# Issuing a weight tile earlier, and cutting modulation pieces into halves, in a two-block f32 transformer kernel

## The chip, the cores and the metric

The kernel runs on one core of a Trainium2 chip. The metric is device time in microseconds (us) of one execution. TensorE is PE in all rows, its weight loads are PEld, VectorE is DVE, ScalarE is ACT, GpSimd is POOL and SyncE is SP. TensorE's clock has two levels, 1.2 and 2.4 GHz; a granted clock of 1.00 in a row is the higher, 0.50 the lower.

## The reference, cut

A sequence of 256 tokens with 1024 features goes through two blocks. The first is a normalisation, a gated mixer, a second normalisation and a mixture of 32 experts of which each token takes four. The second block has two layers whose normalisations are shifted, scaled and gated by modulation vectors, computed as `silu(c) @ ada_w` with `ada_w` of 1024 x 6144 for each layer. Layer 0 mixes with a convolution and a recurrence, layer 1 with stick-breaking attention; each layer ends in an MLP.

```python
proj = h @ w_in                       # 1024 -> qa, ka, va, qb, kb, vb, two gates
lam = exp(sum(lam_q1*lam_k1)) - exp(sum(lam_q2*lam_k2)) + lam_init
out_a = diff_attention(qa, ka, va, lam, lam_init, subln_w)
out_b = chunk_band_attention(qb, kb, vb, rel_bias)
merged = gates[:, :, 0]*(out_a @ w_branch_a) + gates[:, :, 1]*(out_b @ w_branch_b)
...
mod = silu(c) @ ada_w[l] + ada_b[l]   # six vectors of 1024 for each of two layers
```

## The kernel before, in words

**Products.** Every large product is made in f32 precision out of three products of rounded halves. A weight tile of 1024 x 512 (2 MB) is taken in four pairs of 128-row slices. For each pair `wsplit` (L227) has ACT cast the pair (`wh`, L198) and DVE subtract the cast from the pair (`wl`, L199); there are two buffers for `wh` and two for `wl`. `gemm_a` (L238) then makes 12 matmuls of 512 columns from a pair (L254 to L256), 48 from a tile. `gemm_b` (L260) makes 24 matmuls of 256 columns from a pair (L269 to L271), with the weights as the stationary operand.

**Weight tiles.** `wload` (L128, its DMA at L135) brings a tile on SP's queue into a ring of three buffers. The tiles of `w_in` come in the order of their columns: the first (`first_w`, in four parts) and the second (`w_ka`) are issued at the start, the third (`w_va`, columns 1024 to 1535) at L687. Between the second and the third stand SP's small loads: rows of parameters into `raw1` and `raw2` (L158 to L162), `rb` (L163), `lamv` (L166) and two broadcast rows `bcs` (L375). A DMA waits for the one issued eight before it on the same kind of queue; in the order below that is `DMAHW` with a number. The kernel's first products follow the tiles: `qk_block(first_w, 0)`, `qk_block(w_ka, 1)` (tile `qkp`), `v_block(w_va, vA)` (tile `vp`), `qk_block(w_qb, 2)`.

**Uses of the small loads.** PE transposes `raw1` and `raw2` into `pv` (L405, L409), and DVE copies them to `vT` and `abT`. DVE reverses `rb` into `rev`, which POOL's queue writes out (`extd`, L417). DVE and ACT make `lam` from `lamv` (L439 to L447). All of these are released by the end of the first projection. Four passes over `x_tm` with `bcs` (`chain_x`, L419) run between the steps of `v_block`.

**Modulation pieces.** `ada` (L615) is a generator. One piece is 512 columns of `ada_w`: the row `silu_c` against tiles `wa`, into a bank `adp` (L646). Its loads go out on POOL's queue (L622). In the attention stage of layer 1 a tile holds 256 rows (512 KB, `kp` is 2), there are two buffers, and a piece takes four tiles; each tile's load is issued when the tile two before it is used up. Pieces 7 to 11 of layer 1 are made there: `ada1` is advanced once after each of four projections, in the code of the last function, and the fifth piece runs in the code that follows (`proj_out`, then `norm_fm` and the first hidden products of the MLP).

**Order.** The instruction stream of each engine is put in order at build by a scheduler; `tc.issue_after(x)` keeps what stands inside it behind `x`. `fill` holds side work (`chain_x`, `chain_s`) which is advanced by `tick` after each pair.

Of the kernel before, what the change touches and what calls it, by code (L numbers as in the profile page):

```python
# [9 lines left out]
F32 = mybir.dt.float32  # L10
# [62 lines left out]
def tile_kernel(  # L73
# [6 lines left out]
    nc = tc.nc  # L80
# [28 lines left out]
    mark = {}  # L109
# [31 lines left out]
    def wcols(w, c0, ncol, k0=0, kc=8, pool=None, parts=1, pin=False):  # L141
        return wload(w[k0 * 128:(k0 + kc) * 128, c0:c0 + ncol].rearrange("(k p) n -> p k n", p=128),
                     "p (k n) -> p k n", k=kc, pool=pool, parts=parts, pin=pin)
# [3 lines left out]
    raw0 = tmp("raw0", 128)  # L147
    nc.scalar.dma_start(raw0[0:8, :], rows_of(ln_in_g, 8))
    nc.scalar.dma_start(raw0[8:16, :], rows_of(ln_in_b, 8))
    w_ka = wcols(w_in[0], 512, 512)  # L150
    raw1, raw2, rb = [accp.tile([128, 512], F32, tag="a", name=n) for n in ("raw1", "raw2", "rb")]
    raw1, raw2, rb = raw1[:, 0:128], raw2[:, 0:128], rb[0:8, 0:257]
    V.memset(raw1, 0.0)
# [69 lines left out]
                return split(two(xh, c), two(xl, c), v)  # L223
        return f

    hold, ready, deferred = [], [], []

    def wsplit(ws, k, n0):
        if ready:
# [9 lines left out]
    def gemm_a(xh, xl, wk, outs, first=True, last=True):  # L239
        n = len(wk)  # L240
        for i in range(0, n, 2):
            ws, k, n0, _ = wk[i]
            wh, wl = wsplit(ws, k, n0)
            if i == 2:
                while deferred:
                    deferred.pop(0)()
            for j in range(2):
                a = first and i + j == 0
                z = last and i + j == n - 1
                c = wk[i + j][3]  # L250
                for t in range(2):
                    hs = xh[:, c, t * 128:(t + 1) * 128]
                    ls = xl[:, c, t * 128:(t + 1) * 128]
                    T.matmul(outs[t], hs, wh[:, j, :], start=a, stop=False)  # L254
                    T.matmul(outs[t], hs, wl[:, j, :], start=False, stop=False)  # L255
                    T.matmul(outs[t], ls, wh[:, j, :], start=False, stop=z)  # L256
            fill.tick()
# [141 lines left out]
        first_end, first_move = qk_block(first_w, 0)  # L399
    after_v, after_s = mark["V"], mark["S"]  # L400

    with tc.issue_after(first_end):
        vT = const.tile([128, 128], F32, name="vT")
        pv = bank("pv")
        T.transpose(pv[:, 0:128], raw1, ident)  # L405
        V.tensor_copy(vT, pv[:, 0:128])
        abT = const.tile([128, 96], F32, name="abT")
        pv2 = bank("pv2")
        T.transpose(pv2[:, 0:128], raw2, ident)  # L409
        V.tensor_copy(abT, pv2[:, 0:96])  # L410
    spread(ln_in_g, ln_in_b)
    with tc.issue_after(after_v):
        rev = tmp("rev", 384)[0:8]
        V.tensor_copy(rev[:, 0:256], rb[:, 255::-1])
        V.tensor_copy(rev[:, 256:384], rb[:, 0:1].to_broadcast([8, 128]))
        extd = dram.tile([8, 384], F32, name="extd")
        nc.gpsimd.dma_start(extd, rev)  # L417

    def chain_x():  # L419
        for t in range(2):  # L420
            for i, op in enumerate((ALU.mult, ALU.add)):
# [11 lines left out]
        S.activation(bias_a, bias_a, AF.Abs)  # L433
        V.memset(bias_a[0:64, 192:256], -NEG)

    qk_block(w_ka, 1)

    with tc.issue_after(after_v), tc.issue_after(first_move):
        lam = const.tile([128, 1], F32, name="lam")  # L439
        lp = tmp("lp", 128).rearrange("p (a d) -> p a d", a=2)  # L440
        V.tensor_tensor(lp, lamv[:, :, 0, :], lamv[:, :, 1, :], op=ALU.mult)
        le = small("le", 2)
        V.tensor_reduce(le, lp, axis=AX.X, op=ALU.add)
        S.activation(le, le, AF.Exp)
        V.scalar_tensor_tensor(lam, le[:, 0:1], LAM_INIT, le[:, 1:2], op0=ALU.add, op1=ALU.subtract)
        sub8 = const.tile([128, 1], F32, name="sub8")
        V.tensor_scalar(sub8, vT[:, 100:101], 1.0 - LAM_INIT, None, op0=ALU.mult)  # L447
# [151 lines left out]
    def ada(items, late=True):  # L599
        def finish(l, j, acc, tag):  # L600
            v, hf = divmod(j, 2)
            p = bank("ada", tag)
            c = 8 * v + 4 * hf
            for q in range(4):
                T.matmul(p[:, q:q + 1], acc[:, q * 128:(q + 1) * 128], qsel, start=q == 0, stop=q == 3,
                         skip_group_check=True)
            V.tensor_tensor(modT[l][:, c:c + 4], p[:, 0:4], abT[:, 48 * l + c:48 * l + c + 4], op=ALU.add)
            if v in (1, 4) and hf:
                i = v // 3
                V.scalar_tensor_tensor(scl[l][:, i, :], modT[l][:, 8 * v:8 * v + 8], 1.0,  # L610
                                       vT[:, 32 + 16 * i + 8 * l:40 + 16 * i + 8 * l], op0=ALU.add, op1=ALU.mult)

        def flush(h):
            if h[1] // 2 in (2, 5):
                pending.append(h)  # L615
            else:
                finish(*h)

        def load(l, j, i, pin=False):
            w = ada_ring[0](i)  # L620
            r = 128 * ada_ring[2]
            ins = nc.gpsimd.dma_start(w, ada_w_2[l, r * i:r * (i + 1), 512 * j:512 * (j + 1)]  # L622
                                      .rearrange("(k p) n -> p k n", p=128))
            if pin:
                keep(ins)
            return w

        held, got = [], None
        for n, (l, j, tag) in enumerate(items):
            if len(held) > 2:  # L630
                flush(held.pop(0))
            if late and n == len(items) - 1:
                while held:
                    flush(held.pop(0))
                yield
            if got is None:
                got = [load(l, j, i, True) for i in range(2)]
                yield
            kp = ada_ring[2]
            nxt = []  # L640
            pa = bank("adp", tag)
            for i in range(8 // kp):
                for r in range(kp):
                    k = kp * i + r
                    q = 32 * (k % 4)
                    T.matmul(pa[q:q + 32, :], silu_c[:, k:k + 1].to_broadcast([128, 32]), got[i][:, r, :],  # L646
                             start=k < 4, stop=k >= 4, skip_group_check=True)
                if i + 2 < 8 // kp:
                    got.append(load(l, j, i + 2))
                elif ada_ring[1] and n + 1 < len(items):  # L650
                    nxt.append(load(*items[n + 1][0:2], i + 2 - 8 // kp))
            acc = accp.tile([128, 512], F32, tag="a", name="adacc")
            S.copy(acc, pa)
            got = nxt or None
            held.append((l, j, acc, tag))
            yield
        for h in held:
            flush(h)
# [25 lines left out]
        pending.clear()  # L684
        return taken

    w_va = wcols(w_in[0], 1024, 512)  # L687
    fill.add(chain_x())
    v_block(w_va, vA)
    fill.drain()  # L690
# [999 lines left out]
    fill.rate = 1.42  # L1690
    qk_half(0, 0)
    next(ada1, None)
    qk_half(1, 0)
    next(ada1, None)
    keep(S.preload_act_table_set("natural_log_exp_and_others"))
# [3 lines left out]
    qk_half(0, 1)  # L1699
    next(ada1, None)  # L1700
    qk_half(1, 1)
    fill.add(chain_s(1))
    v_half(1)
    fill.drain()
    w_first = proj_out(1, ohl5[:, 0], ohl5[:, 1], w_out_c_2[0], (0, 1), ada1)
    st.close()
# [33 lines left out]
```

## Time and profile before

| | us |
|---|---|
| three runs | 1883.79, 1882.14, 1879.09 |
| median | 1882.14 |
| the profiled execution | 1886.43 |
| its span in the trace | 1884.6 |
| granted TensorE clock over the span | 0.985 |
| busy PE | 1832.9 (97%) |
| busy DVE, ACT, POOL | 842.0, 571.5, 73.9 |

The rows below are from the profiled execution. In a timeline a row has the start, the duration, the engine, the line, the operation and tile, a count of instructions taken together, and in brackets how long the engine stood idle before it and what ended that. PE rows overlap: the time that a matmul takes of PE is the distance from its start to the next one's. In a table by stretch a row has the stretch, its length, the busy time and number of instructions of PE, PEld, DVE, ACT and POOL, the granted clock, the busy share of the 16 DMA engines and what they moved in GB/s.

### The profile page before, as it was taken

How to read it: one execution, taken by the hardware profiler on the slowest of the kernel's cores; microseconds unless marked ns; L12 is line 12 of the kernel's file. 1: busy time of each engine (PE TensorE's matmuls, PEld its weight loads, DVE VectorE, ACT ScalarE, POOL GpSimd, SP SyncE). 2: the span in 40 equal slices, each digit the busy share in tenths (PEclk: the TensorE clock that was granted, in tenths of full speed). 3: DMA queues.
4: the chain of work that ended last, by engine and by line, in shares of the span. 5: the costliest groups of instructions: out<-in, count | busy, mean ns of one | idle time of the engine just before them, and what ended most of it. 6: DMA issues, size and time to landing. Idle time of an engine off the chain costs nothing.

```text
span 1884.6 us, 22815 instructions
## 1 busy us (share of the span) xinstructions
PE 1832.9 (97%) x9419; PEld 1070.7 (57%) x9419; DVE 842.0 (45%) x1521; ACT 571.5 (30%) x934; POOL 73.9 (4%) x101
## 2 busy tenths in 40 slices
PE   6999999999999999999999998999999998999998
PEld 6867743333333333333333333788778865668887
DVE  5775652212131222221222212767755565676666
ACT  3555321011101111101111101554544454564443
POOL 1000000000000000000000000200100011000000
PEclk9999999999999999999999999899999998999999
DMA  8658869999999999999999999774676565434552
GB/s 293 251 192 302 350 250 428 428 427 427 427 428 382 428 427 428 427 428 428 427 428 428 427 428 406 270 256 147 233 263 243 210 232 181 157 134 157 183 202 84
DMA packets 100364, 595.81 MB, mean 316 GB/s; under 512 B 7597, under 2 KB 8066, under 8 KB 75426
## 3 DMA queue, kind: packets, MB, share of 16 engines
q1 hardware_dynamic: 85874, 540.68, 71.2%
q0 software_dynamic: 14352, 53.64, 8.2%
q8 instruction: 75, 1.23, 0.3%
q14 instruction: 31, 0.25, 0.0%
q10 hardware_dynamic: 32, 0.01, 0.0%
HBM read 593.24 MB, written 1.06 MB: 315 GB/s over the span
## 4 chain that ended last, share of the span: by engine, by line
PE 71%; DMA 8%; DVE 3%; issue 3%; ACT 1%; POOL 1%; DVEq 0%; POOLq 0%; ACTq 0%
PE py L980 11%; PE pg L949 10%; PE pu L949 10%; PE hid L285 6%; DMA w<-in_w_exp_in_dram 5%; PE pc L993 4%; PE xg L916 3%; PE acc L254 3%; PE acc L256 3%; PE acc L255 3%; PE hid L287 3%; DMA wa<-in_ada_w_dram 2%; PE adp L646 2%; PE pg L794 1%; PE pu L794 1%
## 5 line engine op out<-in xcount | busy, mean ns | idle before, releaser
L199 DVE TENSOR_TENSOR wl<-w,wh 128x1024 fp32r<-128x1024 f32 x244 | 298.5, 1224 | 217.4 <-ACT wh L198 215.6
L198 ACT CAST wh<-w 128x1024 fp32r<-128x1024 f32 x244 | 256.2, 1050 | 299.7 <-PE acc L256 92.2
L949 PE MATMUL pg<-w,xg 128*64 128x512 f32 x1016 | 260.4, 601 | 1.9 <-DMA w<-in_w_exp_in_dram 1.7
L949 PE MATMUL pu<-w,xg 128*64 128x512 f32 x1016 | 255.6, 592 | 0.0
L980 PE MATMUL py<-w,aTs 128*64 128x512 f32 x1024 | 227.1, 595 | 1.9 <-DMA w<-in_w_exp_out_dram 1.9
L998 DVE TENSOR_TENSOR bcs<-bcs,pc 128x512 f32<-128x512 f32 x124 | 78.1, 683 | 319.5 <-PE pc L993 319.5
L924 DVE TENSOR_SCALAR xg<-xg,gbP 128x128 f32<-128x128 f32 (+1 forms) x68 | 27.3, 401 | 323.9 <-PE xg L916 307.6
L285 PE MATMUL hid<-xhl,wh 128*128 128x512 f32 x448 | 158.7, 398 | 0.0
L949 PEld LDWEIGHTS pu<-w,xg 128*64 128x64 f32 x1016 | 73.0, 137 | 145.8 <-issue 145.8
L980 PEld LDWEIGHTS py<-w,aTs 128*64 128x64 f32 x1024 | 70.7, 137 | 135.6 <-issue 131.8
L949 PEld LDWEIGHTS pg<-w,xg 128*64 128x64 f32 x1016 | 67.0, 137 | 139.3 <-issue 127.8
L287 PE MATMUL hid<-xhl,wl 128*128 128x256 f32 x448 | 125.8, 281 | 0.0
L285 PEld LDWEIGHTS hid<-xhl,wh 128*128 128x128 f32 x448 | 84.2, 188 | 20.7
L254 PE MATMUL acc<-wh,hh 128*128 128x512 f32 x240 | 94.7, 395 | 0.0
L256 PE MATMUL acc<-wh,hh 128*128 128x512 f32 x240 | 93.6, 390 | 0.0
L255 PE MATMUL acc<-wl,hh 128*128 128x512 f32 x240 | 93.6, 390 | 0.0
L974 ACT COPY aTs<-aT 128x512 f32<-128x512 f32 x32 | 18.8, 586 | 231.3 <-PE aT L971 231.3
L287 PEld LDWEIGHTS hid<-xhl,wl 128*128 128x128 f32 x448 | 84.6, 189 | 0.5
L985 ACT COPY ys<-py 128x512 f32<-128x512 f32 x32 | 18.8, 586 | 216.3 <-PE py L980 216.3
L916 PEld LDWEIGHTS xg<-sel,h 128*128 128x128 f32 x544 | 66.7, 196 | 29.6 <-issue 25.1
L993 PE MATMUL pc<-ys,sTs 64*128 64x512 f32 x256 | 79.1, 621 | 0.7 <-ACT ys L985 0.7
L916 PE MATMUL xg<-sel,h 128*128 128x128 f32 (+1 forms) x544 | 72.8, 287 | 2.8 <-DVE sel L907 2.8
(538 smaller groups left out, 2707.9 us busy)
## 6 DMA issues: line engine op xcount, KB each, us to landing
w<-in_w_exp_in_dram SPq DMA_DIRECT2D x125, 2048.0 KB, 18.7
w<-in_w_exp_out_dram SPq DMA_DIRECT2D x63, 2048.0 KB, 17.2
w<-in_mlp_w_dram SPq DMA_DIRECT2D x32, 2048.0 KB, 7.7
wa<-in_ada_w_dram POOLq DMA_DIRECT2D x38, 1024.0 KB, 7.5
w<-in_w_in_dram SPq DMA_DIRECT2D x9, 2048.0 KB, 14.5
w<-in_w_in_ab_dram SPq DMA_DIRECT2D x7, 2048.0 KB, 17.9
w<-in_w_qkv_dram SPq DMA_DIRECT2D x6, 2048.0 KB, 8.1
wa<-in_ada_w_dram POOLq DMA_DIRECT2D x20, 512.0 KB, 4.9
```

What stands on the lines that cost most here:

```text
L198: mark["S"] = S.copy(hi, src).ins
L199: mark["V"] = V.tensor_tensor(lo, src, hi.bitcast(F32), op=ALU.subtract).ins
L254: T.matmul(outs[t], hs, wh[:, j, :], start=a, stop=False)
L255: T.matmul(outs[t], hs, wl[:, j, :], start=False, stop=False)
L256: T.matmul(outs[t], ls, wh[:, j, :], start=False, stop=z)
L285: T.matmul(o.rearrange("p (a t) -> p a t", a=2), wh[:, j, cs], x[:, :, k, :], start=k == 0, stop=False, skip_group_check=True)
L287: T.matmul(o[:, 0:256], wl[:, j, cs], x[:, 0, k, :], start=False, stop=k == 7, skip_group_check=True)
L916: pin(T.matmul(p[:, kc * 128:kc * 128 + w], h1[:, t, 256 * i + r:256 * (i + 1):2], sel[:, t, 0:w], start=t == 0, stop=t == 1))
L949: last = pin(T.matmul(p[64 * hv:64 * hv + 64, :], xg[:, 2 * i + r, a * 64:(a + 1) * 64], w[:, r, b0 + hv * 512:b0 + (hv + 1) * 512], start ...
L980: pin(T.matmul(py[64 * j:64 * j + 64, :], aT[:, r * 128 + i * 64:r * 128 + (i + 1) * 64], w[:, r, j * 512:(j + 1) * 512], start=i == 0 and ...
L993: pin(T.matmul(p, sT[64 * j:64 * j + 64, t * 128:(t + 1) * 128], ys[64 * j:64 * j + 64, :], start=not sums, stop=True))
L998: V.tensor_tensor(f, f, pc[j], op=ALU.add)
```

## The change

The load of the third tile, `w_va`, is issued directly behind that of the second. The uses of the small loads (`vT`, `abT`, `rev`, `extd`, `lam`, `sub8`) are released by the end of the second projection and no longer by the first; `chain_x`, `u_lt`, `ones` and `bias_a` are written earlier in the code. In `ada`, where a tile holds 256 rows, there is a `yield` after the second of four tiles, so that one advance makes half a piece; `gemm_a` advances `midway[0]` at its third pair of four, and two more advances are written out in the stage.

```diff
-    w_ka = wcols(w_in[0], 512, 512)
+    w_ka, w_va = [wcols(w_in[0], c, 512) for c in (512, 1024)]
...
-    hold, ready, deferred = [], [], []
+    hold, ready, deferred, midway = [], [], [], []
...
             if i == 2:
                 while deferred:
                     deferred.pop(0)()
+            if i == 4 and midway:
+                next(midway[0], None)
...
-    with tc.issue_after(first_end):
+    second_end, second_move = qk_block(w_ka, 1)
+    second_v = mark["V"]
+
+    with tc.issue_after(second_end):
         vT = const.tile([128, 128], F32, name="vT")
         pv = bank("pv")
         T.transpose(pv[:, 0:128], raw1, ident)
...
-    spread(ln_in_g, ln_in_b)
-    with tc.issue_after(after_v):
+    with tc.issue_after(second_v):
         rev = tmp("rev", 384)[0:8]
...
-    qk_block(w_ka, 1)
-
-    with tc.issue_after(after_v), tc.issue_after(first_move):
+
+    with tc.issue_after(second_v), tc.issue_after(second_move):
         lam = const.tile([128, 1], F32, name="lam")
...
                 elif ada_ring[1] and n + 1 < len(items):
                     nxt.append(load(*items[n + 1][0:2], i + 2 - 8 // kp))
+                if kp == 2 and i == 1:
+                    yield
...
-    w_va = wcols(w_in[0], 1024, 512)
     fill.add(chain_x())
     v_block(w_va, vA)
...
     qk_half(0, 0)
     next(ada1, None)
+    midway.append(ada1)
     qk_half(1, 0)
     next(ada1, None)
...
     qk_half(1, 1)
+    next(ada1, None)
     fill.add(chain_s(1))
     v_half(1)
+    midway.pop()
     fill.drain()
```

On SP's queue, just behind the second tile, the order before is this (`raw` is `raw1`, and the tile in the last row is `w_va`):

```order
L135 DMA w<-in_w_in_dram 128x8x512 [waits DMAHW0_49]
L158 DMA raw_100<-in_ln_g_dram 8x128 [waits DMAHW1_49,DVE_49]
...
L158 DMA raw_100<-in_hg_norm_dram 4x128 [waits DMAHW7_49]
L158 DMA raw_100<-in_lb_logits_dram 12x128 [waits DMAHW0_49]
...
L375 DMA bcs<-in_ln_in_b_dram 128x1024 [waits DMAHW3_49]
L135 DMA w<-in_w_in_dram 128x8x512 [waits DMAHW4_49]
L718 DMA wr<-in_w_router_dram 128x8x32 [waits DMAHW5_49]
L135 DMA w<-in_w_in_dram 128x8x512 [waits DMAHW6_49,DVE_49]
```

The third tile stood behind nineteen small loads there, of which those from `lb_logits` on wait for a lane that the second tile holds. In the changed kernel the same place reads so:

```order
L135 DMA w<-in_w_in_dram 128x8x512 [waits DMAHW0_49]
L135 DMA w<-in_w_in_dram 128x8x512 [waits DMAHW1_49]
L158 DMA raw_102<-in_ln_g_dram 8x128 [waits DMAHW2_49,DVE_49]
...
L158 DMA raw_102<-in_hg_norm_dram 4x128 [waits DMAHW0_49]
L158 DMA raw_102<-in_lb_logits_dram 12x128 [waits DMAHW1_49]
...
L377 DMA bcs<-in_ln_in_b_dram 128x1024 [waits DMAHW4_49]
L723 DMA wr<-in_w_router_dram 128x8x32 [waits DMAHW5_49]
L724 DMA brt<-in_b_router_dram 128x32 [waits DMAHW6_49]
L135 DMA w<-in_w_in_dram 128x8x512 [waits DMAHW7_49,DVE_49]
```

The third tile went ahead of all small loads, `hg_norm` now waits for the lane of the second tile and `lb_logits` for that of the third, and the last row is the fourth tile (`w_qb`).

On DVE, around the second projection, the order before is this, from the end of `lam`'s sums to the steps of `v_block` (its `wl` rows from the last group on stand beside `x_tm`):

```order
L443 TENSOR_REDUCE le<-lp 128x2
L199 TENSOR_TENSOR wl<-w,wh 128x1024
L432 TENSOR_SCALAR vab<-jp 128x256
L406 COPY vT<-pv 128x128
L410 COPY abT<-pv_327 128x96
...
L199 TENSOR_TENSOR wl<-w,wh 128x1024 x3
L423 TENSOR_TENSOR x_tm<-x_tm,bcs 128x1024
L199 TENSOR_TENSOR wl<-w,wh 128x1024
L423 TENSOR_TENSOR x_tm<-x_tm,bcs 128x1024
```

In the changed kernel the same work stands so on DVE, from the last three pairs of the second projection on:

```order
L199 TENSOR_TENSOR wl<-w,wh 128x1024 x3
L436 COPY rev<-rb 8x256
L437 COPY rev<-rb 8x128
L445 TENSOR_TENSOR lp<-lamv 128x128
L447 TENSOR_REDUCE le<-lp 128x2
L199 TENSOR_TENSOR wl<-w,wh 128x1024
L409 TENSOR_TENSOR x_tm<-x_tm,bcs 128x1024
L429 COPY vT<-pv 128x128
L433 COPY abT<-pv_454 128x96
L451 TENSOR_SCALAR sub_469<-vT 128x1
L199 TENSOR_TENSOR wl<-w,wh 128x1024
L449 SCALAR_TENSOR_TENSOR lam<-le 128x1
```

The uses of the small loads moved from the second projection's steps to the first two pairs of `v_block`.

On PE, in the first projection after the first half piece (`qk_half(1, 0)`, tile `qk5`), the order before is this:

```order
L256 MATMUL qk5_9609<-wh_9610,xhl3_6445 128x512
L254 MATMUL qk5_9608<-wh_9626,xhl3_6445 128x512
L255 MATMUL qk5_9608<-wl_9627,xhl3_6445 128x512
L256 MATMUL qk5_9608<-wh_9626,xhl3_6445 128x512
L254 MATMUL qk5_9609<-wh_9626,xhl3_6445 128x512
L646 MATMUL adp_9589<-wa_9592,silu_c_469 32x512 x2
L255 MATMUL qk5_9609<-wl_9627,xhl3_6445 128x512
L256 MATMUL qk5_9609<-wh_9626,xhl3_6445 128x512
L254 MATMUL qk5_9608<-wh_9626,xhl3_6445 128x512
L646 MATMUL adp_9589<-wa_9596,silu_c_469 32x512 x2
L255 MATMUL qk5_9608<-wl_9627,xhl3_6445 128x512
```

The second half of the piece stood behind 16 of the block's 48 matmuls, its two tiles three matmuls apart. In the changed kernel:

```order
L257 MATMUL qk5_9599<-wl_9617,xhl3_6445 128x512
L258 MATMUL qk5_9599<-wh_9616,xhl3_6445 128x512
L650 MATMUL adp_9589<-wa_9592,silu_c_471 32x512 x2
L650 MATMUL adp_9589<-wa_9596,silu_c_471 32x512 x2
L256 MATMUL qk5_9598<-wh_9640,xhl3_6445 128x512
L257 MATMUL qk5_9598<-wl_9641,xhl3_6445 128x512
```

It stands behind 24 of the 48 now, with its two tiles side by side. In the next block, `v_half(0)`, it moves from behind 18 of 48 to behind 24 in the same way, and it stands directly ahead of the sixteen transposes `qkT` there. The fifth piece, which before stood in the norm and the first hidden products of the MLP, stands in `v_half(1)` and `proj_out`.

## Rows read from the trace of the kernel before

**Rows 1.** Table by stretch (columns as above), the stages that the change touches.

```profile
44.80:59.50 14.70, 14.24 (x49) 11.20 (x50) 10.55 (x9) 5.53 (x7) 0.00 (x0) 0.77 0.71 249
59.50:270.00 210.50, 206.13 (x1182) 150.48 (x1181) 144.21 (x367) 100.55 (x200) 9.25 (x15) 1.00 0.70 263
270.00:1171.00 901.00, 894.35 (x4161) 334.77 (x4162) 208.55 (x431) 98.01 (x191) 4.02 (x8) 0.99 1.00 424
...
1549.20:1567.03 17.83, 15.11 (x60) 9.45 (x56) 5.74 (x6) 5.76 (x9) 2.83 (x4) 0.90 0.66 212
1567.03:1589.10 22.07, 19.13 (x81) 11.55 (x80) 13.41 (x26) 8.03 (x11) 2.83 (x4) 0.85 0.62 203
...
1684.00:1704.40 20.40, 17.23 (x96) 10.64 (x94) 15.36 (x32) 10.77 (x23) 5.81 (x5) 0.92 0.46 155
```

**Rows 2.** Timeline of PE, end of the second projection to the fourth.

```profile
38.78 0.28 PE L271 MATMUL qkp<-xhl,wl 128*128 128x256 f32 x1
44.79 0.80 PE L254 MATMUL vp<-wh,xhl 128*128 128x512 f32 x1 [5.73 <-ACT wh L198]
...
59.24 0.39 PE L256 MATMUL vp<-wh,xhl 128*128 128x512 f32 x1
59.47 0.28 PE L269 MATMUL qkp<-xhl,wh 128*128 128x256 f32 x1
```

**Rows 3.** Timeline of ACT, the first cast of the third tile.

```profile
43.69 1.04 ACT L198 CAST wh<-w 128x1024 fp32r<-128x1024 f32 x1 [9.42 <-DMA w<-in_w_in_dram]
```

**Rows 4.** Timeline of SP's queue: a small load, the third tile, the fourth.

```profile
17.18 0.30 SPq L158 DMA_DIRECT2D raw<-in_lb_logits_dram  x1
...
22.77 0.69 SPq L135 DMA_DIRECT2D w<-in_w_in_dram  x1
...
26.25 13.65 SPq L135 DMA_DIRECT2D w<-in_w_in_dram  x1
```

**Rows 5.** Table by stretch: end of the second tile's transfer, and ahead of the experts.

```profile
14.00:16.00 2.00, 1.94 (x9) 1.65 (x9) 2.00 (x4) 1.01 (x3) 0.00 (x0) 1.00 1.05 386
16.00:18.00 2.00, 2.00 (x13) 2.00 (x12) 0.71 (x2) 0.62 (x1) 0.00 (x0) 1.00 0.27 88
260.00:270.00 10.00, 7.22 (x43) 3.90 (x40) 4.63 (x20) 3.62 (x5) 0.00 (x0) 1.00 0.26 75
```

**Rows 6.** DMA issues from 0 to 60 us: count, size, median us from issue to landing.

```profile
w<-in_w_in_dram SPq DMA_DIRECT2D x5, 2048.0 KB, 20.8
```

**Rows 7.** Waits of PE from 1540 to 1710 us (total, times, longest).

```profile
PE adp L646 <- DMA wa<-in_ada_w_dram: 8.6, 5, 2.9
```

**Rows 8.** Timeline of PE, attention stage of layer 1, its modulation pieces.

```profile
1555.85 1.05 PE L646 MATMUL adp<-wa,silu_c 128*32 128x512 f32 x4 [2.72 <-DMA wa<-in_ada_w_dram]
...
1560.59 0.40 PE L256 MATMUL qk<-wh,xhl 128*128 128x512 f32 x1
...
1567.03 1.06 PE L646 MATMUL adp<-wa,silu_c 128*32 128x512 f32 x8
1574.89 1.92 PE L646 MATMUL adp<-wa,silu_c 128*32 128x512 f32 x4 [2.94 <-DMA wa<-in_ada_w_dram]
...
1581.06 0.40 PE L254 MATMUL v<-wh,xhl 128*128 128x512 f32 x1
...
1585.40 1.03 PE L210 MATMUL qkT<-ident,qk 128*128 128x128 f32 x8
1586.19 0.47 PE L254 MATMUL v<-wh,xhl 128*128 128x512 f32 x1
...
1621.02 1.05 PE L646 MATMUL adp<-wa,silu_c 128*32 128x512 f32 x4 [0.99 <-DMA wa<-in_ada_w_dram]
...
1694.91 1.94 PE L646 MATMUL adp<-wa,silu_c 128*32 128x512 f32 x8
...
1701.59 1.05 PE L646 MATMUL adp<-wa,silu_c 128*32 128x512 f32 x4 [1.39 <-DMA wa<-in_ada_w_dram]
```

**Rows 9.** Tile wa from 1515 to 1720 us, issue to landing.

```profile
DMA to landing us min/median/max: 4.0/5.0/9.3
```

More of the change, by code (lines that the diff above doesn't have):

```diff
@@ L400, in tile_kernel @@
     after_v, after_s = mark["V"], mark["S"]
-    with tc.issue_after(first_end):
[L403 to L410, printed above, removed]
-    spread(ln_in_g, ln_in_b)
-    with tc.issue_after(after_v):
[L413 to L417, printed above, removed]
+    spread(ln_in_g, ln_in_b)
     def chain_x():
@@ L434, in tile_kernel @@
         V.memset(bias_a[0:64, 192:256], -NEG)
-    qk_block(w_ka, 1)
-    with tc.issue_after(after_v), tc.issue_after(first_move):
+    second_end, second_move = qk_block(w_ka, 1)
+    second_v = mark["V"]
+    with tc.issue_after(second_end):
+        vT = const.tile([128, 128], F32, name="vT")
+        pv = bank("pv")
+        T.transpose(pv[:, 0:128], raw1, ident)
+        V.tensor_copy(vT, pv[:, 0:128])
+        abT = const.tile([128, 96], F32, name="abT")
+        pv2 = bank("pv2")
+        T.transpose(pv2[:, 0:128], raw2, ident)
+        V.tensor_copy(abT, pv2[:, 0:96])
+    with tc.issue_after(second_v):
+        rev = tmp("rev", 384)[0:8]
+        V.tensor_copy(rev[:, 0:256], rb[:, 255::-1])
+        V.tensor_copy(rev[:, 256:384], rb[:, 0:1].to_broadcast([8, 128]))
+        extd = dram.tile([8, 384], F32, name="extd")
+        nc.gpsimd.dma_start(extd, rev)
+    with tc.issue_after(second_v), tc.issue_after(second_move):
         lam = const.tile([128, 1], F32, name="lam")
```

## The prediction

> **What bounds the kernel now.** PE is busy for 97% of the span, so I read first where it is not, or is busy at the lower clock. The table by stretch [rows 1] has two such places that the change touches: the third projection, 44.8 to 59.5 us, with a granted clock of 0.77, and the attention stage of layer 1, whose two projections at 1549.2 and 1567.03 run at 0.90 and 0.85. Then I read the timeline of PE for what stands ahead of each.
>
> At the first place PE ends the second projection at 39.06 and starts `v_block` at 44.79, after 5.73 us idle [rows 2]; what it waits for is ACT's cast, and ACT had itself stood for 9.42 us until the third tile landed [rows 3]. That tile was issued at 22.77 [rows 4] and took 20.8 us [rows 6]. So transfer ends last there, and the lower clock behind it is a second loss: 48 matmuls take 14.68 us (44.79 to 59.47), where at the full clock one takes 0.23 (59.24 to 59.47) and 48 take 11.0.
>
> At the second place PE waits for the modulation tiles `wa` five times, 8.6 us in all [rows 7]. The two longest, 2.72 and 2.94, are followed by slow stretches; behind a wait of 0.99 the small products still take 1.05, as at full clock, where at the lower level they take 1.92 [rows 8].
>
> Between the two places the time goes through PE. From 59.5 to 270 it is busy for 206.13 of 210.50 us [rows 1]. The expert stage from 270 on is a transfer stage (DMA share 1.00, 424 GB/s), but ahead of it the DMA moves 75 GB/s only [rows 5]: its stream starts when PE gets there. Time saved ahead of it should pass through.
>
> **Third tile first.** The second tile is landed by about 16.5, since the traffic falls from 386 to 88 GB/s there [rows 5]. A further 2.1 MB behind it at 386 GB/s takes 5.4 us: the third tile lands near 22 in place of 43.7. Its cast then waits for split buffers alone, and PE goes from the second projection into the third with no idle time. What PE takes on at that seam are the two transposes of `raw1` and `raw2`; eight of that size take 0.79 [rows 8], so two take 0.2 to 0.3, and they only move. The block ends near 39.06 + 0.3 + 11.0 = 50.4 in place of 59.47: **9.1 us**.
>
> What is late next? DVE: within the block it has four `wl` and four passes over `x_tm`, 10.55 us busy with nine instructions in this stretch [rows 1], and now eight small operations of `vT`, `rev`, `lam`, beside 11.0 of PE. The order puts at most one `x_tm` between two `wl`, and the first `wl` stands ahead of the block, so I take no stall; a stall of one pass, 1.2, is the bound. The small loads from `lb_logits` on wait for the third tile and not the second: `lb_logits` leaves near 22.5 in place of 17.18, the fourth tile near 28 to 31 in place of 26.25 [rows 4]. They are now wanted only when the second tile is split, and ACT's last cast of it ends at 34.27 (43.69 − 9.42, [rows 3]), so 5.4 us later costs nothing. The fourth tile is wanted at 50. POOL's loads (`extd`, the first `wa`) stand behind `rev` and so behind that split too, so for some 5 us the fourth tile is alone on the DMA; if it took the 20.8 us of the third tile all the same [rows 6], it would land at 49 to 52, up to 2 us late. I take the term as 9.1, with 5 to 9.5 as bounds.
>
> **Pieces in halves.** Before, the loads for the second half of the first piece start when its first half is done (1549.20, [rows 1]) and PE uses them at 1555.85: 6.65 us. PE had 16 matmuls to do meanwhile, 3.7 us. In the changed order there are 24, 5.5 us, so a wait near 1.1 is left, or none if the tiles come at the median of 5.0 [rows 9]. Each half has the same distance ahead of it in these two blocks. The second point is that two tiles now stand side by side: eight small products together take 1.06, four alone take 1.05 [rows 8], so a half costs one microsecond in place of two.
>
> First block, from the end of the first half piece: 48 matmuls 11.0, the second half 1.0, two waits of 1.1, 14.2 in place of 17.83: 3.6. Second block: 11.0, two halves 2.0, one wait 1.1, sixteen transposes 2 x 0.79 = 1.6, so 15.7 in place of 22.07: 6.4. By parts, 2.72 and 2.94 of waits, and lower-clock stretches (1555.85 to 1560.59, 4.74 us for four matmuls and eight small products, and 1574.89 to 1581.06, 6.17 us for five and eight) go. If none of the three waits is left the two blocks give 13; if each is 1.8, 8. I take **10**.
>
> Pieces three and four: the waits left of 8.6 are 0.99 and, by difference, 8.6 − 2.72 − 2.94 − 0.99 − 1.39 = 0.6. Attention work stands between the halves there, so they are far enough apart; waits and pairing make 1.6 to 3.6, and some halves are parted by side work. I take **2**. Fifth piece: in the norm and the first hidden products it takes 1.94 at the lower clock, two times 1.05, and a wait of 1.39 [rows 8], 5.4 in all; its two halves cost 2.1 in `v_half(1)` and `proj_out`. So 3.3 at most, and less, since PE had nothing else to do in part of that time and will then start the hidden products at the lower clock for longer: I take **1**, bounds −2 and 3.3. Part two is 13, bounds 7 and 17.
>
> **A rule beside it.** The trace shows the two long waits followed by the lower clock, and the wait of 0.99 not [rows 8]. The Trainium skill, page "TensorE: Matmul & The Clock Gate", section "A second HAM failure mode: psum-queue depth-cycling", says that frequent short idling between groups of matmuls makes the clock swing between its two levels. By that rule ten halves with a wait each would do worse than the five long waits before; that is the slower rival below. The trace so far, with 0.99, does not bear it out.
>
> **Sum.** 9.1 + 13 = 22.1. The profiled execution took 1886.43, 4.3 above the median of the three runs; of its time 1.8 lies around the span and stays. Against itself that is 1886.43 − 22.1 = 1864.3, and by the median 1882.14 − 22.1 = **1860**. I forecast against the median.
>
> **Rivals.**
>
> *The waits stay.* The three waits in the first two blocks remain at 2.7, the tiles coming as late as they did, and the clock falls behind each as it did behind 2.72. That fall cost 4.74 − 4 x 0.23 − 2 x 1.05 = 1.7 beyond the work in its stretch. The two blocks then give 10 − 3 x (2.7 − 1.1 + 1.7) = 0, part two the remaining 3, and the time is 1882.14 − 9.1 − 3 = 1870. For it: a weight tile and `wa` share the DMA, and 9.3 us to landing occurs [rows 9]. Against: the distance grew by eight matmuls, and behind 0.99 the clock stayed. With waits of 1.1 and the fall alone it would be 1865, within my range.
>
> *The first part halves.* The fourth tile, with `wa` and `extd` beside it, lands as slowly as the third did and PE stands 2 us at 50.4, with a lower clock of the size of 14.68 − 11.0 = 3.7 behind it: 9.1 − 5.7 leaves 3.4, time 1866. Against: the fourth tile leaves before POOL's loads. If the shift were swallowed by the expert stage instead (DMA share 1.00), the first part gives 0 and the time is 1869; against it the 75 GB/s ahead of that stage [rows 5].
>
> *Slower.* Every one of the ten halves waits for its own loads as the first did, 2.72, with the fall of 1.7 behind it: 44 us in place of 8.6 and falls of 1.7 and (6.17 − 5 x 0.23 − 2 x 1.05) = 2.9, 13.2 together, a loss of 31, less 9.1: 1904. It needs, on the mean of the ten halves, (13.2 + 9.1)/10 = 2.2 us to come out slower at all. For it: ten waits in place of five, and no half is loaded farther ahead than before. Against: the distance is 5.5 in place of 3.7, and the median landing 5.0 [rows 9].
>
> *No effect.* The scheduler could put the moved work back where it stood; the order shown above speaks against that, and it would give 1882.
>
> **How the numbers follow.** Forecast 0.70; waits stay 0.11; first part halved or swallowed 0.10; slower 0.04; no effect or several of the small terms at their worst together 0.05. Low end: 9.5 + 17 = 26.5, beyond which only a gain that I don't see would lead, 1856, and 4 us for the runs' own scatter (1879.09 to 1883.79): 1852. High end: 5 + 8 = 13, 1869; this takes in the first part's rivals and most of the other. Outside is about 0.17. A measurement of this kernel can tell some 0.3%, 5.6 us, from no change. Faster by more holds for the forecast, both middle rivals and a little of the last: 0.92; within it 0.04; slower 0.04.
>
> **What would show it.** In the changed profile: the third tile's cast ahead of the end of the second projection, no idle time of PE there, clock 1.00 to 60 us, and the fourth projection starting near 50.4. In the attention stage: waits of PE for `wa` of 1.1 at most, no matmul at the lower clock ahead of the norm, first block near 14, second near 16. The forecast is wrong if the fourth tile ends a wait at 50, if small products of 1.92 stand in the attention stage, or if the start of the experts has not moved by about 9.

## The result and the profile after

The changed kernel takes 1865.09 us (median of three, 1864.15 to 1865.48), the kernel before 1882.14: ratio 0.9911, 95% interval 0.9898 to 0.9925. That is 17.0 us less, clear of the 0.3% that can be told from no change, within the stated range, and 5 us short of the 1860 forecast.

The timeline of PE at the first seam, the counterpart of [rows 2], shows the two moved transposes (`pv`), the third projection (`vp`) and the start of the fourth:

```profile
37.35 0.27 PE L428 MATMUL pv<-ident,raw 128*128 128x128 f32 x1
...
37.49 0.47 PE L256 MATMUL vp<-wh,xhl 128*128 128x512 f32 x1
...
48.27 0.39 PE L258 MATMUL vp<-wh,xhl 128*128 128x512 f32 x1
48.49 0.28 PE L271 MATMUL qkp<-xhl,wh 128*128 128x256 f32 x1
```

No row has a wait in brackets. The third projection takes 11.0 us in place of 14.68, and the fourth starts 10.98 us earlier than in [rows 2].

The waits of PE in the attention stage of layer 1, from 1530 to 1700 us (total, times, longest), answer [rows 7]; the timeline of the pieces answers [rows 8]:

```profile
PE adp L650 <- DMA wa<-in_ada_w_dram: 2.6, 3, 1.6
PE rb L1271 <- POOL nrs L1269: 1.4, 2, 1.1
PE pl L1667 <- ACT Eh L198: 1.2, 2, 0.9
```

```profile
1544.85 1.05 PE L650 MATMUL adp<-wa,silu_c 128*32 128x512 f32 x4 [0.74 <-DMA wa<-in_ada_w_dram]
1546.13 1.05 PE L650 MATMUL adp<-wa,silu_c 128*32 128x512 f32 x4 [0.23 <-DMA wa<-in_ada_w_dram]
...
1552.78 1.05 PE L650 MATMUL adp<-wa,silu_c 128*32 128x512 f32 x4
...
1555.45 1.05 PE L650 MATMUL adp<-wa,silu_c 128*32 128x512 f32 x4 [1.62 <-DMA wa<-in_ada_w_dram]
...
1562.09 1.06 PE L650 MATMUL adp<-wa,silu_c 128*32 128x512 f32 x8
```

Waits for `wa` fell from 8.6 to 2.6 us. Two of the halves still find their second tile missing and are multiplied in two lots of four (1.05 each), where a half whose tiles are both there takes 1.06 for eight. The table by stretch (columns as in [rows 1]) has the first two blocks of the stage:

```profile
1538.44:1552.78 14.34, 13.37 (x58) 9.07 (x57) 5.67 (x6) 6.97 (x10) 2.83 (x4) 1.00 0.78 287
1552.78:1570.62 17.84, 16.16 (x82) 10.95 (x81) 13.40 (x26) 6.75 (x10) 2.83 (x4) 1.00 0.68 221
```

Their granted clock is 1.00, where [rows 1] has 0.90 and 0.85, and they take 14.34 and 17.84 us where those took 17.83 and 22.07.

The two traces differ by 21.4 us (spans 1884.6 and 1863.2), not by 17. Cut at seven starts of PE rows that both have (distances in us; the "last norm" starts with its first `rb`, the "end" is the start of the last PE row, 5.0 us ahead of the span's end):

| stretch | before | changed | difference |
|---|---|---|---|
| first to fourth projection | 45.91 | 34.97 | −10.9 |
| fourth projection to the attention stage | 1477.63 | 1477.76 | +0.1 |
| attention stage to its first scores (`pz`) | 52.01 | 44.37 | −7.6 |
| to the second value projection | 46.24 | 45.58 | −0.7 |
| to the last norm | 56.00 | 59.07 | +3.1 |
| last norm to the end | 188.24 | 182.97 | −5.3 |

The fourth and fifth stretches do not hold the same work before and after. Sixteen one-column products `ada`, which take 1.8 us, stand in the fifth before and in the fourth in the changed kernel. The timelines of PE, before and then changed:

```profile
1679.94 1.95 PE L605 MATMUL ada<-qsel,adacc 128*128 128x1 f32 x16
```

```profile
1614.39 1.95 PE L609 MATMUL ada<-qsel,adacc 128*128 128x1 f32 x16
1616.20 0.49 PE L256 MATMUL v<-wh,xhl 128*128 128x512 f32 x1
1616.52 0.61 PE L257 MATMUL v<-wl,xhl 128*128 128x512 f32 x1
1616.92 0.63 PE L258 MATMUL v<-wh,xhl 128*128 128x512 f32 x1
```

For the same work the fourth stretch got 2.5 us shorter and the fifth 4.9 longer. The last rows show a second thing: without any wait of PE ahead, the clock fell here (rows of 0.63 in place of 0.39, up to 1619.9). In a second profile of the changed kernel it did not, and the fifth stretch is 57.47 there, 1.6 less.

Two questions are open here: which part gives what, and why the medians differ by less than the traces.

### The profile page after: what moved, and what is told of

Same layout as the page of the kernel before. It is cut to its first block, busy times and chain, and to the rows that moved or that the text cites. A ratio compares the mean times of both kernels' runs of the same rounds, so it can differ in the third digit from the quotient of the medians.

```text
span 1863.2 us, 22812 instructions
## 1 busy us (share of the span) xinstructions
PE 1821.0 (98%) x9419; PEld 1067.9 (57%) x9419; DVE 841.9 (45%) x1521; ACT 571.6 (31%) x934; POOL 73.8 (4%) x101
## 3 DMA queue, kind: packets, MB, share of 16 engines
HBM read 593.24 MB, written 1.06 MB: 319 GB/s over the span
## 4 chain that ended last, share of the span: by engine, by line
PE 76%; DMA 5%; DVE 3%; ACT 1%; issue 1%; POOL 0%; DVEq 0%; POOLq 0%; ACTq 0%
PE pg L954 11%; PE py L985 11%; PE pu L954 10%; PE hid L287 6%; PE pc L998 4%; PE xg L921 3%; PE acc L256 3%; PE acc L258 3%; PE acc L257 3%; PE hid L289 3%; DMA w<-in_w_exp_in_dram 2%; DMA w<-in_w_exp_out_dram 2%; PE adp L650 2%; PE pg L799 1%; PE pu L799 1%; DMA wa<-in_ada_w_dram 1%
```

## The experiments

All ratios are against the kernel before on the same chip. Four kernels were measured together first.

**The first part alone.** The edit takes the second part out of the changed kernel:

```diff
-            if i == 4 and midway:
-                next(midway[0], None)
...
-                if kp == 2 and i == 1:
-                    yield
...
-    midway.append(ada1)
...
-    next(ada1, None)
     fill.add(chain_s(1))
     v_half(1)
-    midway.pop()
```

> The kernel before with the first part alone: third weight tile issued behind the second, uses of the small loads behind the second projection, pieces whole as before. Theory (the two parts act at separate places and add; the first is worth the 9.1 us of the sum): the fourth projection starts near 50 us or, where the first matmuls run at the full clock, near 48.5 in place of 59.5, no idle time of PE ahead of the third, and the time is 1873 (1882.1 - 9.1). Rival (the expert stage or the lower clock takes part of it back): the fourth projection starts as early, but the expert stage's end has moved by 5 or less, 1877 to 1882.

1874.8 us, ratio 0.9962 (0.9951 to 0.9974): 7.2 us, the interval 4.9 to 9.2. The fourth projection starts 34.99 us after the first, as in the changed kernel, PE does not wait ahead of the third, and the stretch up to the attention stage takes no more than before (1475.1). So the gain passes through the expert stage.

**The second part alone.**

```diff
-    w_ka, w_va = [wcols(w_in[0], c, 512) for c in (512, 1024)]
+    w_ka = wcols(w_in[0], 512, 512)
...
+    w_va = wcols(w_in[0], 1024, 512)
     fill.add(chain_x())
     v_block(w_va, vA)
```

with the blocks that use the small loads back in their old places.

> The kernel before with the second part alone: pieces in halves, weight tile and small loads as before. Theory (the traces of the two kernels show 10.6 us from the attention stage of layer 1 on: 3.4 and 4.2 in its first two blocks, 0.3 by the fourth piece, 2.7 lost up to the last norm, 5.3 won back from there): 1871.5, with the idle 5.7 us ahead of the third projection as before. Rival (the medians differ by 17.05, and 9.1 of that is the first part, so that the second is worth 8): 1874. If the parts don't add, 1876 or more.

1874.31, ratio 0.9964 (0.9951 to 0.9977): 6.8 us, the interval 4.3 to 9.2. The rival's 1874 is the one that came. From the attention stage to the end its trace has 45.41 + 45.58 + 57.52 + 183.02 = 331.5 us, the changed kernel's 332.0 and that of before 342.5: the trace says 11 where the runs say 7. The two parts make 7.2 + 6.8 = 14.0 against 16.4 for both at once (next run): inside the intervals they add. By the medians of these runs each part is worth more behind the other: the second takes the kernel with the first from 1874.8 to 1865.36, 9.4 us, and the first takes the kernel with the second from 1874.31 to 1865.36, 9.0.

**The changed kernel again** and **the kernel before again**, without an edit.

> The changed kernel once more beside the others. If the difference of the medians (17) is the true one: ratio 0.991, 1865. If that of the two traces (21.4) is nearer, the ratio comes out at 0.9885 to 0.990.

> The kernel before once more, for a second profile of it. Theory (part of the 4.3 us by which its profiled execution lay above its median is the state of the clock, which does not follow from the program): the time is 1879 to 1884, and the stretches 13.5 to 17.5 us (first matmuls at 0.21 apart in the first profile, 0.12 in the changed kernel's) or 1534 to 1537 (modulation piece of 3.11 us) differ from the first profile. Rival (they follow from the program): both read as in the first profile, and the time is 1886.

The changed kernel: 1865.36, ratio 0.9913 (0.9896 to 0.9929), which speaks for the difference of the medians. The kernel before: 1885.24 in its profiled execution, beside a median of 1881.4 over 18 runs (1877.15 to 1885.57). Both stretches differed as the theory said (the piece at 1534 took 1.92, not 3.11, and the first matmuls ran at the full clock up to 15.3 us and at the lower one from there); but the time lay outside the theory's 1879 to 1884 and near the rival's 1886. A profile of this kernel has twice been of one of its longest executions. The timelines of PE for the two pieces of the first two blocks differ from profile to profile. The first profile has, beside the two rows of [rows 8] behind the waits (1555.85 and 1574.89), these for the second lots:

```profile
1558.29 1.92 PE L646 MATMUL adp<-wa,silu_c 128*32 128x512 f32 x4
...
1578.32 1.92 PE L646 MATMUL adp<-wa,silu_c 128*32 128x512 f32 x4
```

This second profile has:

```profile
1555.48 1.92 PE L646 MATMUL adp<-wa,silu_c 128*32 128x512 f32 x4 [3.14 <-DMA wa<-in_ada_w_dram]
...
1558.90 1.92 PE L646 MATMUL adp<-wa,silu_c 128*32 128x512 f32 x4
...
1575.31 1.92 PE L646 MATMUL adp<-wa,silu_c 128*32 128x512 f32 x4 [2.45 <-DMA wa<-in_ada_w_dram]
...
1578.74 1.05 PE L646 MATMUL adp<-wa,silu_c 128*32 128x512 f32 x4
```

and in a profile of the kernel before with four idle products at its very start (the last experiment below):

```profile
1554.78 1.92 PE L651 MATMUL adp<-wa,silu_c 128*32 128x512 f32 x4 [2.72 <-DMA wa<-in_ada_w_dram]
...
1558.02 1.05 PE L651 MATMUL adp<-wa,silu_c 128*32 128x512 f32 x4
...
1572.99 1.05 PE L651 MATMUL adp<-wa,silu_c 128*32 128x512 f32 x4 [2.25 <-DMA wa<-in_ada_w_dram]
...
1574.87 1.05 PE L651 MATMUL adp<-wa,silu_c 128*32 128x512 f32 x4
```

For four products a 1.05 is the full clock, a 1.92 the lower one. In the first profile the clock was down in three of these four places, in the second in three others, here in one. The waits at each place are the same to 0.7 us. So how much the clock takes there differs from one execution to the next. That it falls is nearly certain: in the five profiles with whole pieces and their loads (these three, the first part alone, and the next experiment) it fell behind nine of the ten waits, which are 2.25 to 3.37 us long; the exception is the shortest. From the attention stage to its first scores these five take 52.0, 52.0, 48.4, 53.8 and 50.3 us, 51.3 on average; the four with halves and their loads, in the places of the change, 44.2 to 45.4, 44.6 on average. The runs' scatter fits: their standard deviation within a measurement is 2.4 us over 90 runs with whole pieces and their loads and 1.4 over 33 with halves, though one kernel with halves (halves farther apart, below) has 2.4 over four. Other stretches scatter too: the one ahead of the attention stage by 4 us over all profiles.

**The first part without the move of the uses.** Against the kernel before, only this:

```diff
-    w_ka = wcols(w_in[0], 512, 512)
+    w_ka, w_va = [wcols(w_in[0], c, 512) for c in (512, 1024)]
...
-    w_va = wcols(w_in[0], 1024, 512)
```

> The first part without the move of the uses: third tile behind the second, but the transposes, rev and lam still released by the end of the first projection. Theory (the move is needed, since the small loads now come 5 us later): PE or DVE wait for the small loads within the second projection for 1 to 3 us, and the time is 1876 to 1878, against 1874.8 with the move. Rival (the scheduler finds other work and the move is worth nothing): 1875, no wait of PE above 0.5 us between 24 and 38 us.

1883.1, ratio 0.9997 (0.9985 to 1.001): nothing is left of the 7 us. The theory had the mechanism, but not its size. The timeline of DVE, then that of PE, then a table by stretch:

```profile
26.69 0.28 DVE L414 COPY rev<-rb 8x256 f32<-8x256 f32 x1 [2.90 <-DMA rb<-in_rel_bias_dram]
...
31.26 0.29 DVE L441 TENSOR_TENSOR lp<-lamv 128x128 f32<-128x128 f32 x1 [3.88 <-DMA lamv<-in_lambda_k_dram]
...
31.79 1.22 DVE L199 TENSOR_TENSOR wl<-w,wh 128x1024 fp32r<-128x1024 f32 x1
```

```profile
33.06 0.58 PE L271 MATMUL qkp<-xhl,wl 128*128 128x256 f32 x1 [5.29 <-DVE wl L199]
```

```profile
33.00:36.00 3.00, 2.94 (x13) 2.94 (x14) 1.59 (x7) 2.04 (x5) 0.90 (x1) 0.50 1.08 397
```

DVE stands before `rb` and `lamv`, which the third tile has pushed back; the split of the second tile's first pair (31.79) is queued behind them, PE waits 5.29 us for it, and the clock falls to 0.50. The third projection starts 32.96 us after the first, later than before (31.23). The wait has moved from the third tile to the second projection. Without the move of the uses the first part gains nothing; the move alone, with the tile in its old place, was not run.

**No loads for the pieces.** The pieces of the attention stage use their first two tiles over and over, once in the kernel before and once in the changed one; the values are not the reference's.

```diff
-                    got.append(load(l, j, i + 2))
+                    got.append(load(l, j, i + 2) if kp != 2 else got[i])
...
-                    nxt.append(load(*items[n + 1][0:2], i + 2 - 8 // kp))
+                    nxt.append(load(*items[n + 1][0:2], i + 2 - 8 // kp) if kp != 2 else got[i])
```

> The kernel before in which the modulation pieces of the attention stage use the first two tiles over and over; the other loads of that stage are left out, so nothing there waits for a load. Theory (whole pieces lose by waits for their loads and the lower clock behind them, 8.6 us of waits and some 5 of falls in the first profile): 1869 to 1873, and no matmul of the stage at the lower clock up to the last norm. Rival (they lose by their place and by standing apart on PE): 1877 or more.

> The changed kernel with the same loads left out. Theory (2.6 us of waits for loads are what is left, with no fall of the clock behind them): 1862 to 1863. Rival (the waits left cover for something else, such as the attention chain's steps on ACT and DVE): 1865, as with the loads.

Before: 1862.98, ratio 0.9892 (0.9874 to 0.9910), 20 us, more than the theory's 9 to 13. Changed: 1860.29, ratio 0.9875 (0.9856 to 0.9895), some 5 below the changed kernel where 2.6 was expected. The table by stretch of the first has the two blocks at the full clock, and the timeline shows a whole piece as one row:

```profile
1547.00:1573.40 26.40, 25.21 (x134) 18.20 (x133) 18.21 (x31) 13.11 (x18) 0.00 (x0) 1.00 0.41 146
```

```profile
1547.16 1.92 PE L646 MATMUL adp<-wa,silu_c 128*32 128x512 f32 x16
```

Sixteen small products of a piece together take 1.92 at the full clock, where parted as 8 + 4 + 4 they took 1.06 + 1.05 + 1.05 = 3.2. Late loads thus cost a third thing besides the wait and the clock: the products are parted, 1.2 us for each of five pieces. In the code the four products of two tiles go to four different groups of 32 columns (`q = 32 * (k % 4)`), those of one tile to two. In the changed kernel what the missing loads give is 2.6 of waits and 2 x 1.0 for the two halves that were multiplied in two lots, 4.6: from the attention stage to its first scores it is 39.7 in place of 44.4.

**The fifth piece back towards the norm.** In the changed kernel no half falls into the middle of the last two projections:

```diff
     qk_half(0, 1)
     next(ada1, None)
+    midway.pop()
     qk_half(1, 1)
     next(ada1, None)
     fill.add(chain_s(1))
     v_half(1)
-    midway.pop()
```

> The changed kernel with no half piece in the middle of the last two projections, so that the fifth piece falls back towards the norm as in the kernel before. Theory (the fifth piece costs 5.3 us in the norm and behind it, and 2.7 in the last projection and the output projection): 1867 to 1868. Rival (the norm has idle time that takes the piece for nothing, and the steps of the attention chain do better without it): 1863.

1866.47, ratio 0.9911 (0.9897 to 0.9926), against 0.9911 and 0.9913 with the piece ahead; the medians differ by 1 us, inside the intervals. Its trace shows the exchange: from the last norm on 186.77 in place of 182.97, with a wait again, and 43.62 + 56.79 in place of 45.58 + 59.07 (or 57.47, without the fall of the clock) ahead of it.

```profile
1681.10 1.05 PE L650 MATMUL adp<-wa,silu_c 128*32 128x512 f32 x4 [1.37 <-DMA wa<-in_ada_w_dram]
```

The place of the fifth piece is worth nothing that these runs can tell.

**Halves farther apart.** In the changed kernel the third pair's advance becomes a list of pairs for each block:

```diff
-            if i == 4 and midway:
+            if midway and i in midway[1]:
...
+    midway[:] = [ada1, (4,)]
     qk_half(0, 0)
-    next(ada1, None)
-    midway.append(ada1)
+    midway[1] = (2,)
     qk_half(1, 0)
     next(ada1, None)
+    midway[1] = (6,)
...
     v_half(0)
-    next(ada1, None)
+    midway[1] = (2,)
     qk_half(0, 1)
     next(ada1, None)
+    midway[1] = (4,)
     qk_half(1, 1)
     next(ada1, None)
+    midway[1] = (2, 6)
```

> The changed kernel with the half pieces farther apart at the start: the first in the middle of the first projection of the attention stage, then 36 matmuls between halves in place of 24 up to the fourth. Theory (what the changed kernel still loses in the first two blocks is the waits for loads, 2.6 us, and two tiles that come one after the other and so are multiplied apart, 2 us): no wait of PE for these loads, and 1861. Rival (the loads take longer when they are issued elsewhere, and the waits move along): 1865.

1863.69, ratio 0.9889 (0.9873 to 0.9906). Theory and rival were both half right: the first two blocks lost their waits (41.3 us to the first scores in place of 44.2 to 44.4), but a half farther on found its loads missing, with 24 matmuls of its projection ahead of it; the clock fell while it was multiplied (the 1.48), and that stretch took 47.47 in place of 45.58:

```profile
1610.80 1.05 PE L650 MATMUL adp<-wa,silu_c 128*32 128x512 f32 x4 [0.73 <-DMA wa<-in_ada_w_dram]
...
1613.56 1.48 PE L650 MATMUL adp<-wa,silu_c 128*32 128x512 f32 x4 [1.71 <-DMA wa<-in_ada_w_dram]
```

**The same with the first half of the fourth piece one pair earlier.**

```diff
-    midway[1] = (4,)
+    midway[1] = (2,)
     qk_half(1, 1)
```

> The kernel with the half pieces farther apart, in which the first half of the fourth piece moves one pair forward in the last key projection, since its second half waited 2.4 us for two loads behind only 24 matmuls. Theory (only the distance counts): the second half waits for nothing, the first for 0.7 us at most, and the time is 2 us below the kernel with the wider spacing, 1861 to 1862, and 3 to 4 below the changed kernel. Rival (waits of this size are taken up by the attention chain's own waits): 1864.

1861.84, ratio 0.9890 (0.9873 to 0.9906). As the theory said. This wait is gone (0.8 us are left in the whole stage), and the stretch takes 44.41:

```profile
1609.99 1.06 PE L650 MATMUL adp<-wa,silu_c 128*32 128x512 f32 x8
```

All four runs (1860.11 to 1862.83) lie below all three of the changed kernel's first measurement, but not below all five of its second (from 1862.82). From the attention stage to the last PE row the trace has 328.4 us against 332.0 and 330.7 in the two profiles of the changed kernel. A gain of some 3 us is likely but not shown: the intervals of the ratios overlap, and the kernels ran on different chips.

**Idle products ahead of the start.** Four f32 products of a zero tile, ahead of PE's first use at 6.9 us:

```diff
+    warm = tmp("warm")
+    keep(V.memset(warm, 0.0))
     ident = const.tile([128, 128], F32, name="ident")
...
+    pw = bank("pw")
+    for _ in range(4):
+        T.matmul(pw, warm[:, 0:128], warm, start=True, stop=True)
     vT0 = const.tile([128, 16], F32, name="vT0")
```

It was tried on the kernel with wider spacing and on the kernel before, since the two profiles of the changed kernel differ at the start. The timelines of PE, the second profile first (0.21 us between starts, the lower clock), then the first (0.12):

```profile
14.90 0.41 PE L271 MATMUL qkp<-xhl,wh 128*128 128x256 f32 x1
15.11 0.41 PE L272 MATMUL qkp<-xhl,wh 128*128 128x256 f32 x1
```

```profile
14.71 0.28 PE L271 MATMUL qkp<-xhl,wh 128*128 128x256 f32 x1
14.83 0.28 PE L272 MATMUL qkp<-xhl,wh 128*128 128x256 f32 x1
```

> The same, with four idle f32 products of a zero tile on PE ahead of its first use at 6.9 us; their output is not used. Theory (the state of the clock at the first products, which cost 2.5 us in one profile of the changed kernel and nothing in the other, follows from PE's idle time ahead of them): the first projection runs at the full clock, the third starts 24 us after the first, and the time is 1 us below the one without. Rival (it does not): no difference, or 0.5 to 1 us more for the products themselves.

> The kernel before with the same four idle products. Theory (there the start lies hidden behind the load of the third tile): the third projection starts at 44.5 to 45 us as before, and the time is 1881 to 1882. Rival (a faster start is worth something there too): 1880 or less. It is also a third profile of the stage with whole pieces: if the lower clock behind its waits is a matter of chance, one of the two slow stretches there is absent or shorter than in the first profile (4.74 and 6.17 us).

With wider spacing: 1864.31, ratio 0.9898 (0.9881 to 0.9914), no gain. The timeline and the table by stretch:

```profile
10.04 1.09 PE L212 MATMUL xT<-ident,x_tm 128*128 128x128 f32 x8 [0.75 <-DVE x_tm L365]
13.41 0.80 PE L273 MATMUL qkp<-xhl,wh 128*128 128x256 f32 x2 [2.28 <-ACT xhl L200]
```

```profile
12.60:14.00 1.40, 0.59 (x2) 0.50 (x2) 1.40 (x4) 1.26 (x3) 0.00 (x0) 0.50 1.10 313
```

The products raise the clock early: the transposes `xT` take 0.14 us each in place of 0.23. PE then stands idle for 2.28 us in place of 1.0, since `xhl` from ACT comes hardly sooner (the first projection starts at 13.41, without the products at 13.68), and the first projection starts at the lower clock, as it does without them (0.80 for its first two products in both):

```profile
13.68 0.80 PE L271 MATMUL qkp<-xhl,wh 128*128 128x256 f32 x2 [0.98 <-ACT xhl L198]
```

The kernel before: 1882.06, ratio 0.9996 (0.9984 to 1.0009), the third projection at 44.5 whatever the start did, as expected: there the start is hidden behind the third tile.

## Why the prediction was right, and where it was off

**The seam, 9.1.** Right, and by its own steps: the third tile was there in time, PE did not wait, the block took 11.0, DVE made no stall, the fourth tile was not late. The first part alone measures 7.2 (4.9 to 9.2), and 9.0 by medians behind the second part. The trace has 10.9, because the first projection ran at the full clock in that profile and not in the one of before; in the second profile of the changed kernel it did not, and the fourth projection starts 37.48 after the first, 8.4 less than before. Of the eight profiles with the tile ahead and the uses moved, two had the fast start. The prediction did not see that the idle 5.73 us had been hiding the start: what the clock costs there now shows. The column of the granted clock does not show it: [rows 5] has 1.00 from 14 to 18 us in the kernel before, where the products start 0.21 us apart up to 17.4, as at the lower clock.

**Passing through.** Right. The stretch from the fourth projection to the attention stage is 1477.6 and 1477.8; over all profiles it scatters from 1474.6 to 1478.7.

**The step that was off: the pieces in halves, 13, by the term for the first two blocks, 10; and the sum was taken from the median.** The mechanism is right: the two blocks ran at the full clock, and the waits fell from 8.6 to 2.6. By the traces the part is worth 10.5 and not 13. The first two blocks gave 7.7 where 10 was taken: of waits there were 0.97 and 1.62, less than three times 1.1, but the second tile came apart from the first in two halves, and the products beside each other that the sum had counted as one microsecond took two. Pieces three and four gave the 2 that was taken for them: 0.7 in the table, 2.5 with the `ada` products counted where they were before.

The two falls of the clock, 1.7 and 2.9, were counted as if every execution had them. Nearly all have falls there, of different cost; over five profiles the stretch takes 0.7 us less on average than in the first. So this is a small part of what was missed.

The traced execution lay 4.3 above the median, and the prediction took its losses from the median. Against the execution's own time the same sum gave 1864.3, and 1865.09 came; the prediction gave both figures and chose the other. That 1864.3 came so close is in part luck, since the seam gave 1.8 more in the trace than was taken and the pieces 2.5 less. The 4.3 are also the difference between the traces' 21.4 and the medians' 17.0. Other profiles show where some of it lies: 1.1 at the seam (first to fourth projection 44.8 us on average in four others with the tile in its old place, 45.9 in this one), 0.9 from the attention stage on (341.6 on average over the five with whole pieces, 342.5 in this one). The rest is not located. For the pieces alone the runs give 6.8 (4.3 to 9.2), and 9.4 by medians behind the first part, where the profiles give 10.2 on average (341.6 against 331.4); what makes up this difference is open.

**The fifth piece, 1.** The terms were 5.4 gained behind the norm and 2.1 paid ahead of it. The trace has 5.3 gained and 4.9 paid, 3.1 in the table and the 1.8 of `ada`. The payment is 3.0 for the products, whose second half is parted by side work into two lots, and 1.6 for the fall of the clock at 1616.5, which the second profile does not have. The gain holds a lower clock too, the 1.94 for eight products [rows 8], which two of the other four profiles with whole pieces do not have. Moving the piece back changed the time by 1 us, within the intervals.

**The rivals.** "The waits stay" fell: 2.6 us are left, and no fall behind 1.62. "The first part halves" fell with the fourth projection's start. "Slower" and the rule beside it fell: the two blocks run at 1.00, and the short waits of the halves did not make the clock swing in the profiles of the changed kernel. One thing expected did not come: a stage without matmuls at the lower clock ahead of the norm; but the fall there, at 1616.5, followed the sixteen one-column products and no wait. The move of the small loads' uses, which the prediction priced as work that only moves, decides the first part: without it there is no gain at all. A slip in the range: its high end takes 8 for the second part, whose own bound was 7; that would be 1870 in place of 1869.

## What to carry to other kernels

Take a sum that was read from one trace against that execution's own time, and look in a second profile what the same stretch costs: what the lower clock takes behind the same wait differs from one execution to the next. When two traces are compared by stretches, check that the same work stands in each. When a large transfer is issued ahead of small ones, move what uses the small ones as well, and look at what is queued behind those uses on their engine. A side task fed by loads wants as much other work between its parts as its loads take to land, everywhere along the stage, and it wants a part's tiles all there when the part starts.

## What the runs showed of the hardware

- Behind waits of PE of 2.25 to 3.37 us the clock fell nine times out of ten (five profiles, two places of the same stage); what it cost differed. Waits of 1.14 to 1.16 us stand in all fourteen profiles at two norms (for `rb`): behind 8 of these 28 the lower clock began within a microsecond, in the changed kernel behind neither in the first profile and behind both in the second. Behind a wait of 1.62 it stayed up, behind one of 1.71 it fell.
- The clock also fell with no wait: in three profiles (the first of the changed kernel, the second of the kernel before, and the kernel before with idle products) the lower clock began 0.3 to 0.4 us behind the sixteen one-column products `ada`, and in others it did not. What decides is not shown.
- At the very start the granted clock in the rows reads 1.00 (14 to 18 us in the kernel before, [rows 5]) where products start 0.21 us apart, the distance of the lower clock; there the distances tell the level.
- Four idle products ahead of the start made the transposes faster (0.14 us each in place of 0.23), and PE then waited the longer for ACT (2.28 us in place of 1.0); the first projection ran at the lower clock as it did without them.
- Small products of the modulation take about one microsecond for four and for eight, and 1.92 for sixteen, at the full clock: the eight of two tiles side by side cost no more than the four of one.
